# Loading a quarter of the keys onto both partition halves with one transfer, and both parts of the queries with one transfer, in a stick-breaking attention layer

## The chip, the cores and the metric

The kernel runs on one core of a Trainium2 chip. The metric is the device time of one execution in microseconds (us). The time given is the median of a few executions, and one further execution was recorded by the hardware profiler. All views quoted below are of that profiled execution.

## What is computed

One layer of a decoder trunk over 1024 tokens of width 2048, in float32. The input is normalized, multiplied by one big input matrix, and split into two groups of heads. Sixteen stick-breaking heads (`sb`) and sixteen sliding-window heads (`sw`, with four key/value heads) each attend, their outputs are normalized, gated and multiplied by one output matrix, and a normalized result is added to the input. The part that the change touches is the scores of the attention, `z = q k`:

```
u = rmsnorm(h, norm_pre)
q_sb, k_sb, v_sb, z_sb, q_sw, k_sw, v_sw, z_sw = split(u @ w_in)
# stick-breaking head:
z = einsum('bqhd,bshd->bhqs', q_blk, kh) * scale
log_1m_beta = where(before, log_sigmoid(-z), 0)
suffix = cumsum(log_1m_beta, reverse) - log_1m_beta
w = where(before, exp(log_sigmoid(z) + suffix), 0)
out = einsum('bhqs,bshd->bqhd', w, vh)
# then: o = rmsnorm(o) * silu(z), y = concat(o_sb, o_sw) @ w_out, h + rmsnorm(y)
```

## The kernel before

**The matrix engine's work.** Every float32 product is made of products of a high and a low part of each factor: a value is split into `hi` (rounded to the matrix engine's type) and `lo` (what is left), and a projection adds `hi*hi`, `hi*lo` and `lo*hi`. A projection (`proj`, L452 on) makes one block of 128 output columns of the input matrix for 1024 tokens, in four groups of weights. Each group is 256 KB, is loaded into a tile `wraw` (three buffers, L131), and is split by ScalarE (L133) and VectorE (L135). 52 projections stand in a list `work`; the attention is done in between.

**Attention between the projections.** After each three matmuls of a projection, `step()` may place one stage of one attention unit: `s1` makes the scores `z` and the weights on ScalarE, GpSimd and VectorE, `s2` transposes them on TensorE, `s3` multiplies them with the values. The places are decided while the program is written, by a running sum of matmul times (`pe_time`), with a period of 4.7 for a stick-breaking unit. A stick-breaking head has ten units: four query quarters `a`, each with the key quarters `c` from `a` to 3. A unit's transfers (`prep`) are placed when three units or fewer stand before it (`AHEAD = 3`).

**How keys and queries get onto the chip's partitions.** A projection of queries or keys leaves its high and its low part in device memory, `qd` and `kd`, each of shape [2 parts, 128 rows, 1024 tokens]; a head has 64 of the 128 rows. For the scores, TensorE works on 128 partitions at once: a query tile `q` has the high part of the queries on partitions 0 to 63 and the low part on 64 to 127. The key tiles `kh` (high part) and `kl` (low part) have the same 64 rows twice, on 0 to 63 and again on 64 to 127. One matmul with `kh` and one with `kl` then give all four products. There is one tile `kh` and one tile `kl` in the whole program; `load_k` (L478) refills a quarter, 256 tokens, at a time. It does so with four transfers: for each of the two parts, one for each partition half (L484). The stick-breaking queries come with two transfers, one for each part (L521), twice per head. The sliding-window queries (L603) come with two transfers of [64 rows, 2 heads, 256 tokens] each and are not touched by the change, but the sliding-window heads use the same `load_k`.

**What sets the order.** All these transfers are issued by the SyncE queue (SP), in program order, with the weights' loads (L131), the spills of queries and keys (L376, L377), the attention's output (L495, L497), and the background jobs. A background job (L224 to L229) loads two pieces of the output matrix into `row_sw` or `bg`, adds them on GpSimd (L227) and stores the sum `wsum`. A tile framework places the waits and, where the code does not force an order, orders each engine's instructions by its own estimates. Matmuls and background jobs are kept in the order in which they are written. The framework gives each transfer one of eight completion semaphores in turn, and a transfer first waits until the one eight before it has landed.

After the last projections comes the output stage: seven products of half-size matrices (L907), with sums and splits on the other engines. No key or stick-breaking query is loaded there.

## Time and profile before

| what | value |
|---|---|
| median of 3 runs | 1807.02 us (1804.5 to 1808.76) |
| the profiled execution | 1807.31 us |
| its span, from the first to the last instruction | 1805.6 us |
| TensorE busy in the span | 1780.6 us (99%) |
| VectorE, ScalarE, GpSimd busy | 1245.8, 789.6, 496.0 us |
| bytes moved by the DMA engines | 312.48 MB |
| matrix engine's mean granted clock | 0.998 |

In the quoted lines PE is TensorE, DVE is VectorE, ACT is ScalarE, POOL is GpSimd, and SPq is SyncE's queue, which issues the transfers. `x64` is a count. In a group's line the first pair after the bar is the total busy time in us and the mean of one in ns; after the next bar stands the idle time of the engine just before these instructions, in us, with what ended most of it. A view of windows cuts the span into stretches and gives each engine's busy time, the granted clock, and the share of its 16 DMA engines' time in which they were moving packets. "Landing" is the time at which a transfer's completion is signalled.

The stick-breaking units run from 512 us, where the first scores of pair 0 are made, to 1424 us, where the last of pair 7 are made. There are eight pairs of heads.

### The profile page before, as it was taken

Reading aid. Unit: us, or ns where it says so; the run is one execution under the profiler, and the core shown is the slowest. Engines: PE = TensorE matmul, PEld = TensorE weight load, DVE = VectorE, ACT = ScalarE, POOL = GpSimd, SP = SyncE. Lnnn points to the kernel's source line nnn. Section 1 sums busy time; section 2 is a strip of 40 time slices with the busy share of each in tenths; the row PEclk is TensorE's granted clock in tenths of the full one; section 3 lists DMA queues with packets and bytes.
Section 4 is the critical chain, followed back from the end, with each engine's and each line's share of the span. In section 5 each row is a group of like instructions: output and inputs, shape, how many; then the busy total and the mean of one; then the engine's idle time right before and its main releaser. Section 6 shows DMA issues by size and latency. Waiting matters only on the chain. (4 is left out here: it accounts for less than half of the span.)

```text
span 1805.6 us, 27329 instructions
## 1 busy us (share of the span) xinstructions
PE 1780.6 (99%) x9046; PEld 1492.2 (83%) x9046; DVE 1245.8 (69%) x1984; ACT 789.6 (44%) x1696; POOL 496.0 (27%) x648
## 2 busy tenths in 40 slices
PE   8999999999999999999999999999999999999997
PEld 7788888888888888888888888888888887888886
DVE  7558852588567688587776787767858657746867
ACT  7335531355344444344443444434435434445433
POOL 0011121211213333133232322232313225504523
PEclk9999999999999999999999999999999999999999
DMA  7548675576747657466556564454435386634485
GB/s 230 193 138 219 199 223 148 167 210 206 224 124 199 182 164 195 142 182 184 175 163 185 153 183 129 137 169 139 151 91 140 98 258 210 198 105 129 143 250 184
DMA packets 203884, 312.48 MB, mean 173 GB/s; under 512 B 24640, under 2 KB 84192, under 8 KB 203616
## 3 DMA queue, kind: packets, MB, share of 16 engines
q1 hardware_dynamic: 201680, 307.60, 57.7%
q10 hardware_dynamic: 2064, 3.15, 0.5%
q8 instruction: 72, 1.18, 0.3%
q14 instruction: 68, 0.56, 0.1%
HBM read 219.42 MB, written 91.23 MB: 172 GB/s over the span
## 5 line engine op out<-in xcount | busy, mean ns | idle before, releaser
L543 DVE TENSOR_TENSOR_SCAN m_sb<-m_sb,m_sb,zero 128x257 f32<-128x257 f32 x192 | 157.3, 857 | 46.9 <-ACT m_sb L530 46.4
L530 ACT ACTIVATE m_sb<-z_sb 128x512 f32<-128x512 f32 x160 | 96.1, 601 | 132.1 <-PE z_sb L122 119.9
L546 DVE TENSOR_TENSOR b_sb<-b_sb,m_sb 128x512 f32<-128x512 f32 x160 | 129.0, 806 | 20.5 <-POOL b_sb L536 9.0
L540 DVE TENSOR_TENSOR_SCAN m_sb<-m_sb,mask 128x256 f32<-128x256 f32 x128 | 117.4, 953 | 35.2 <-ACT m_sb L530 34.5
L907 PE MATMUL y<-wohi,x 128*128 128x512 f32 x448 | 140.8, 390 | 0.0
L562 DVE TENSOR_TENSOR wl_sb<-wt_sb,wh_sb 128x512 fp32r<-128x512 f32 (+1 forms) x160 | 100.7, 631 | 57.7 <-ACT wh_sb L561 57.0
L561 ACT CAST wh_sb<-wt_sb 128x512 fp32r<-128x512 f32 (+1 forms) x160 | 86.9, 543 | 111.6 <-PE wt_sb L126 109.3
L907 PE MATMUL y<-wohl,x 128*128 128x512 f32 x576 | 132.8, 389 | 2.7 <-DVE wohl L773 2.7
L907 PEld LDWEIGHTS y<-wohl,x 128*128 128x128 f32 x576 | 108.0, 188 | 25.5 <-DVE wohl L773 3.1
L122 PE MATMUL p_qsb<-xh,whi_qsb 128*128 128x512 f32 x256 | 104.5, 408 | 0.0
L122 PE MATMUL p_ksb<-xh,whi_ksb 128*128 128x512 f32 x256 | 104.4, 408 | 0.0
L122 PE MATMUL p_zsw<-xh,whi_zsw 128*128 128x512 f32 x256 | 104.3, 407 | 0.0
L122 PE MATMUL p_vsb<-xh,whi_vsb 128*128 128x512 f32 x256 | 102.9, 402 | 0.0
L122 PE MATMUL p_zsb<-xh,whi_zsb 128*128 128x512 f32 x256 | 102.9, 402 | 0.0
L623 ACT ACTIVATE L_sw<-L_sw,nm_sw 128x256 f32<-128x256 f32 (+1 forms) x128 | 62.6, 490 | 91.6 <-DVE nm_sw L618 88.5
L122 PE MATMUL p_zsw<-xh,wlo_zsw 128*128 128x512 f32 x256 | 101.0, 394 | 0.0
L122 PE MATMUL p_ksb<-xh,wlo_ksb 128*128 128x512 f32 x256 | 100.9, 394 | 0.0
L122 PE MATMUL p_qsb<-xh,wlo_qsb 128*128 128x512 f32 x256 | 100.8, 394 | 0.0
L122 PE MATMUL p_ksb<-xl,whi_ksb 128*128 128x512 f32 x256 | 100.7, 394 | 0.0
L122 PE MATMUL p_zsw<-xl,whi_zsw 128*128 128x512 f32 x256 | 100.7, 393 | 0.0
L122 PE MATMUL p_vsb<-xh,wlo_vsb 128*128 128x512 f32 x256 | 100.7, 393 | 0.0
L122 PE MATMUL p_qsb<-xl,whi_qsb 128*128 128x512 f32 x256 | 100.6, 393 | 0.0
(242 smaller groups left out, 4974.3 us busy)
## 6 DMA issues: line engine op xcount, KB each, us to landing
row_sw<-in_w_out SPq DMA_DIRECT2D x80, 256.0 KB, 4.2
bg<-in_w_out SPq DMA_DIRECT2D x80, 256.0 KB, 4.5
woraw<-wsum SPq DMA_DIRECT2D x80, 256.0 KB, 3.3
kh<-kd SPq DMA_DIRECT2D x160, 64.0 KB, 3.3
kl<-kd SPq DMA_DIRECT2D x160, 64.0 KB, 3.1
wsum<-row_sw SPq DMA_DIRECT2D x40, 256.0 KB, 2.6
wsum<-bg SPq DMA_DIRECT2D x40, 256.0 KB, 3.1
q_sw<-qd SPq DMA_DIRECT2D x64, 128.0 KB, 3.6
```

The costliest lines, as they stand in the source:

```text
L122: tc.keep_in_program_order(nc.tensor.matmul(ps, a, b, start=start, stop=stop))
L530: nc.scalar.activation(m[:, :, 1:257], z, AF.Sigmoid, scale=-SCALE)
L540: nc.vector.tensor_tensor_scan(m[:, tb, 1:257], m[:, tb, 1:257], mask[:, P - P * tb:P - P * tb + 256], m[:, tb, 0:1], ALU.mult, ALU.max)
L543: nc.vector.tensor_tensor_scan(m[:, tb, :], m[:, tb, :], zero.to_broadcast([P, 257]), prev[:, tb, 256:257], ALU.mult, ALU.max)
L546: nc.vector.tensor_mul(beta, beta, m[:, :, 0:256])
L561: nc.scalar.copy(wh[:, :k], pt[:, :k])
L562: nc.vector.tensor_sub(wl[:, :k], pt[:, :k], wh[:, :k].bitcast(F32))
L623: nc.scalar.activation(L[:, hh, :n], L[:, hh, :n], AF.Exp, bias=nm[:, hh:hh + 1], accum_out=sm[:, hh:hh + 1])
L907: nc.tensor.matmul(ps, xt[:, a, tcols], w[b][:, cols], start=first and n == 0, stop=last and n == 2)
```

## The change

Each quarter of each key part is now loaded by one transfer. Its source names the 64 rows twice, by an outermost step of 0 with a count of 2, and its destination is all 128 partitions. The queries of a stick-breaking head are loaded by one transfer too. Its source is the two parts of `qd`, 64 rows each, and its destination is all 128 partitions.

```
 def load_k(src, row, c):
     ...
     cols = slice(c * 256, (c + 1) * 256)
     for r in range(2):
-        for d in range(2):
-            nc.sync.dma_start(kk[r][d * HD:(d + 1) * HD, cols].bitcast(F32), src[r, row:row + HD, cols])
+        one_k = src[r, row:row + HD, cols]
+        twice = bass.AP(one_k.tensor, one_k.offset, [[0, 2]] + list(one_k.ap))
+        nc.sync.dma_start(kk[r][:, cols].bitcast(F32), twice)
...
             if a // 2 not in head:
                 qs = head[a // 2] = at.tile([P, 512], F32R, tag="q", name=f"q_{nm}")
-                for i in range(2):
-                    nc.sync.dma_start(qs[i * HD:(i + 1) * HD, :].bitcast(F32),
-                                      qd[pair][i, row:row + HD, (a // 2) * 512:(a // 2 + 1) * 512])
+                nc.sync.dma_start(qs.bitcast(F32), qd[pair][:, row:row + HD, (a // 2) * 512:(a // 2 + 1) * 512])
```

The source of a key transfer is now the access pattern [2 with step 0][64 rows with step 1024][256], that of a query transfer [2 with step 131072][64 rows with step 1024][512]; the destination is [128 partitions] in both. Before, both sides were [64 rows] or [64 partitions]. The bytes that move are the same. The program issues 1505 transfers on SP before and 1313 after: 192 fewer, 160 of them key transfers and 32 query transfers. TensorE, VectorE and GpSimd keep their instructions in the same order; on ScalarE two neighbours change places. TensorE has 97 fewer instructions that only wait, 357 instead of 454.

SP's order moves at some places, because the framework counts fewer transfers. The first is the first load of keys, for the first sliding-window group, near 80 us. Before (`kd_81` is the first spilled key block, `x2` two transfers in a row, `wraw_qsw_1` the second group of weights of a query projection):

```order
L484 DMA kh<-kd_81 64x256 x2
L484 DMA kl<-kd_81 64x256 x2
L484 DMA kh<-kd_81 64x256 x2
L484 DMA kl<-kd_81 64x256 x2
L484 DMA kh<-kd_81 64x256 x2
L131 DMA wraw_qsw_1_1014<-in_w_blk 128x512
L484 DMA kl<-kd_81 64x256 x2
L484 DMA kh<-kd_81 64x256 x2
L484 DMA kl<-kd_81 64x256 x2
L376 DMA qd_65<-hi_qsw_0_840 128x512
```

The same place after:

```order
L485 DMA kh<-kd_81 128x1x256
L485 DMA kl<-kd_81 128x1x256
L485 DMA kh<-kd_81 128x1x256
L485 DMA kl<-kd_81 128x1x256
L485 DMA kh<-kd_81 128x1x256
L485 DMA kl<-kd_81 128x1x256
L485 DMA kh<-kd_81 128x1x256
L485 DMA kl<-kd_81 128x1x256
L131 DMA wraw_qsw_1_1014<-in_w_blk 128x512
L376 DMA qd_65<-hi_qsw_0_840 128x512
```

Sixteen transfers have become eight, and the load of the weights, which stood behind ten of sixteen, now stands behind all eight. The second place is in the stick-breaking heads, where a head's first two quarters of keys are loaded (near 865 us; `wsum`, `row_sw` and `bg` belong to background jobs). Before:

```order
L131 DMA wraw_ksb_1_9545<-in_w_blk 128x512
L484 DMA kh<-kd_76 64x256 x2
L484 DMA kl<-kd_76 64x256
L229 DMA wsum_6_162<-row_sw 128x512
L484 DMA kl<-kd_76 64x256
L224 DMA row_sw<-in_w_out 128x512
L225 DMA row_sw<-in_w_out 128x512
L131 DMA wraw_ksb_2_9619<-in_w_blk 128x512
L131 DMA wraw_ksb_3_9718<-in_w_blk 128x512
L484 DMA kh<-kd_76 64x256 x2
L484 DMA kl<-kd_76 64x256 x2
```

The same place after:

```order
L131 DMA wraw_ksb_1_9443<-in_w_blk 128x512
L485 DMA kh<-kd_76 128x1x256
L485 DMA kl<-kd_76 128x1x256
L229 DMA wsum_6_162<-row_sw 128x512
L224 DMA row_sw<-in_w_out 128x512
L225 DMA row_sw<-in_w_out 128x512
L131 DMA wraw_ksb_2_9517<-in_w_blk 128x512
L131 DMA wraw_ksb_3_9611<-in_w_blk 128x512
L485 DMA kh<-kd_76 128x1x256
L485 DMA kl<-kd_76 128x1x256
```

Nothing but the number and the shape of the key transfers changes here: the store of the background job now follows the last key transfer instead of standing ahead of it, and the loads around keep their places.

## The prediction, made before the changed kernel was run

> **What bounds the kernel now.** I read the page first. Its head, its first row and its account of the DMA engines:

> ```profile
> span 1805.6 us, 27329 instructions
> ...
> PE 1780.6 (99%) x9046; PEld 1492.2 (83%) x9046; DVE 1245.8 (69%) x1984; ACT 789.6 (44%) x1696; POOL 496.0 (27%) x648
> ...
> DMA packets 203884, 312.48 MB, mean 173 GB/s; under 512 B 24640, under 2 KB 84192, under 8 KB 203616
> ## 3 DMA queue, kind: packets, MB, share of 16 engines
> q1 hardware_dynamic: 201680, 307.60, 57.7%
> q10 hardware_dynamic: 2064, 3.15, 0.5%
> ```

> TensorE is busy for 1780.6 of 1805.6 us; only 25 us can be won at all while its matmuls stay. The view of waits, for TensorE, says whom it waits for:

> ```profile
> PE f0a L122 <- ACT whi_f L308: 5.8, 1, 5.8
> PE y L907 <- DVE wohl L773: 2.7, 1, 2.7
> PE wt_sw L126 <- DVE L_sw L629: 2.4, 4, 1.1
> PE vt_vsw L126 <- DVE v_vsw L396: 1.9, 1, 1.9
> PE o_sb L122 <- DVE wl_sb L562: 1.6, 3, 0.9
> PE o_sw L122 <- ACT ot_sw L493: 0.7, 1, 0.7
> PE y L907 <- DVE wolo L773: 0.3, 1, 0.3
> PE y L907 <- DVE wolast L773: 0.2, 1, 0.2
> ```

> No line names a transfer, of keys or of anything else. The first is the start of the program; the other seven sum to 9.8 us. The remaining 9.4 us of the 25 I take for the end of the program, where the last rows are scaled and stored. The groups of the scores' matmuls, which are the readers of the changed transfers, confirm it:

> ```profile
> L122 PE MATMUL z_sb<-kl,q_sb 128*128 128x256 f32 x320 | 83.0, 281 | 0.0
> L122 PE MATMUL z_sb<-kh,q_sb 128*128 128x256 f32 x320 | 82.9, 281 | 0.0
> ```

> Idle before them is 0.0 us, though each head's first scores now follow on instructions that only wait for a key transfer. So the 97 waits that the change takes from TensorE cost nothing now.

> **The change part by part.** First what it removes. The view of the tiles gives what SP pays for an issue (minimum, median, maximum in ns):

> ```profile
> L484 SPq DMA_DIRECT2D kh<-kd x160: 444/566/2131, 79.3 to 1373.7; - x160
> L521 SPq DMA_DIRECT2D q_sb<-qd x64: 444/587/1341, 460.7 to 1376.2; - x64
> ```

> 192 issues fewer at about 0.57 us free 109 us of SP's queue. None of it is on the path: TensorE waits for no transfer. I count 0, and if the cover were gone a head would gain at most its eight key issues, 4.5 us.

> The bytes stay, so the question is how a new transfer is spread over the 16 DMA engines. The trace of before has no transfer like it. Its packet count shows what it has: 1505 transfers on SP and one on ACT, with 16 little completion packets each, are 24096; the loads of the small tables (256 rows of 32 B, 288 of 64 B) are 544 more; the sum is the 24640 under 512 B in the page, to the packet. So every transfer of before ran on all 16 engines, and every one has an outermost count of 128, 64 or 32. The new ones have an outermost count of 2 on the source side. The two halves cannot be joined into one count of 128 there, since the step between them (0 for keys, 131072 for queries) is not the step between rows. What divides a transfer by its outermost count would give each half to one engine: two engines for the whole.

> [...]

> Price of a megabyte on one engine, from the two queue rows: 57.7% of 16 engines' 1805.6 us is 16669 us for 307.60 MB, 54.2 us per MB; 0.5% is 144 us for 3.15 MB, 45.9 us per MB. A key transfer is 128 rows of 1 KB, 0.131 MB; half of it, on one engine, takes 3.0 us (by 45.9) to 3.55 us (by 54.2). A query transfer is 128 rows of 2 KB and takes 6.0 to 7.1 us on each of its two engines. A pair of heads has 16 and 4 of these: 72 to 85 us on the two engines. Now against the room there is. The view of windows, cut at the first scores of each pair; the last two columns are the share of the DMA engines' time and GB/s:

> ```profile
> 512.40:629.00 116.60, 116.60 (x626) 98.87 (x625) 82.86 (x117) 51.93 (x99) 33.33 (x59) 1.00 0.63 169
> 629.00:747.10 118.10, 116.88 (x626) 98.83 (x625) 88.90 (x117) 51.36 (x98) 40.19 (x67) 1.00 0.64 179
> 747.10:864.10 117.00, 116.61 (x625) 98.82 (x624) 85.84 (x117) 51.43 (x98) 37.08 (x63) 1.00 0.60 174
> 864.10:980.50 116.40, 116.40 (x626) 98.87 (x625) 81.80 (x113) 50.64 (x97) 35.59 (x62) 1.00 0.58 173
> 980.50:1098.60 118.10, 118.10 (x630) 99.62 (x629) 88.30 (x121) 53.57 (x101) 35.33 (x61) 1.00 0.53 153
> 1098.60:1215.00 116.40, 116.40 (x626) 98.77 (x625) 82.25 (x113) 51.39 (x96) 33.62 (x58) 1.00 0.51 152
> 1215.00:1331.40 116.40, 116.40 (x626) 98.86 (x625) 83.05 (x113) 50.49 (x96) 34.76 (x59) 1.00 0.47 142
> 1331.40:1424.90 93.50, 93.50 (x512) 79.76 (x511) 77.21 (x108) 46.84 (x89) 24.48 (x47) 1.00 0.39 104
> ```

> Share times length is what an engine is busy: 73.5, 75.6, 70.2, 67.5, 62.6, 59.4, 54.7 and 36.5 us. From each I take the old share of keys and queries (3.15 MB over 16 engines at 54.2: 10.7 us) and add 72. The two engines then need 134.8, 136.9, 131.5, 128.8, 123.9, 120.7 and 116.0 us in the first seven windows, 18.2, 18.8, 14.5, 12.4, 5.8, 4.3 and 0 us more than the windows have; the last, with one head's keys, has room. The sum is 74 us.

> Every other load has a sixteenth of its bytes on each engine, so it lands only when these two have got to it: the weights and background jobs are late with the keys. What is late next is TensorE. That it has a lead shows in SP's timeline and in TensorE's:

> ```profile
> 905.94 1.09 SPq L484 DMA_DIRECT2D kh<-kd  x2
> 907.12 1.28 SPq L484 DMA_DIRECT2D kl<-kd  x2
> ...
> 925.99 0.28 PE L122 MATMUL z_sb<-kh,q_sb 128*128 128x256 f32 x1
> ```

> A quarter of the keys is issued 20 us before its scores. Two transfers of 3.0 us leave about 14 us, spent once and refilled only in a window with room, so I don't deduct it.

> Bounds: the low end takes the other loads at 45.9 too (the old 73.5 becomes 62.8 x 0.847 = 53.2 without keys, and so on); then 8.6, 8.9, 5.4 and 3.7 us are over in four windows, 27 us in all. The high end takes the new transfers at 54.2, 13.2 us more a window: 166 us. I take the value between, since the row of q10 stems from one large transfer with little beside it, as two engines that lag behind the other fourteen have, and the rest runs in crowds as now. Earlier, in the sliding-window heads, 32 key transfers (of 3.0 us, 96 us over some 370 us) fit: I count 0. The weights moved behind eight key transfers near 80 us wait up to 24 us there, once; a few us of it may show, inside the range.

> The profiled execution took 1807.3 us, 0.3 over the median of the runs. 1807 + 74 = 1881.

> **The rivals.** *Spread over 16 engines after all.* If the division goes by the 128 partitions of the destination, or by the rows, a key transfer lands like one of the present kind:

> ```profile
> kh<-kd SPq DMA_DIRECT2D x160, 64.0 KB, 3.3
> q_sb<-qd SPq DMA_DIRECT2D x64, 128.0 KB, 3.8
> ```

> Then the SP time saved lies beside TensorE's work and the time is 1807, not slower. For it: all transfers seen use 16 engines. Against it: none seen has an outermost count below 16. It decides at 16 completion packets per new transfer.

> *Two engines, but hidden.* At the low prices and with the lead spent, 27 us shrink to 13 or nothing: 1807 to 1820. Against it: the first two windows are over by 18 us each, more than the lead.

> *More than the queue's sum, by the engines behind the loads.* GpSimd already waits for background loads, with the attention's masks behind in the same queue:

> ```profile
> 865.01 1.28 POOL L227 TENSOR_TENSOR row_sw<-row_sw 128x512 f32<-128x512 f32 x1 [8.09 <-DMA row_sw<-in_w_out]
> 866.25 1.01 POOL L536 TENSOR_SCALAR_AFFINE_SELECT b_sb<-b_sb 128x512 f32<-128x512 f32 x1
> ```

> The view of that line in the windows says how often:

> ```profile
> L227 POOL TENSOR_TENSOR bg<-bg x24: 1285/1657/1732, 531.6 to 1064.0; 128x512 f32<-128x512 f32 x24
> L227 POOL TENSOR_TENSOR row_sw<-row_sw x23: 1282/1299/1749, 546.6 to 1050.1; 128x512 f32<-128x512 f32 x23
> ...
>   DMA row_sw<-in_w_out: 47.2, 8
>   DMA bg<-in_w_out: 27.1, 8
> ```

> 16 of 47 sums wait for their load. If each waits for two key transfers more, 6 us, and all of it reaches TensorE on top of the queue's sum, that is 96 us: 1977. Against it: TensorE waiting also gives the two engines time, so the two sums overlap.

> *A gain.* All of TensorE's inner waits are 9.8 us and none is for a transfer; a reordered neighbour could win a part: 1803 at best.

> **How the numbers follow.** Two engines and a queue that overflows: 0.66, 1834 to 1973 (27 to 166 us), 1881 the likeliest. The worse sum on top: 0.08. Two engines but hidden: 0.09, half of it visible. Sixteen engines: 0.15, nearly all within 0.2%. A gain: 0.02. About 0.2%, 3.6 us, is what a measurement of this kernel can tell from no change, since its runs lie 4.3 us apart. Slower is 0.66 + 0.08 + 0.05 = 0.79, no change 0.04 + 0.14 = 0.18, faster 0.02 + 0.01 = 0.03. The range runs from 1806, which keeps most of the unchanged cases in, to 1975, the high bound; outside are the worse sum and the lower half of the unchanged cases, under 2 in 10. The likeliest case's own range is 1834 to 1973.

> **What would show it right or wrong.** Little packets under 512 B: 24640 less 192 x 16 is 21568 if a new transfer still runs on 16 engines, and 14 x 192 fewer, 18880, if on two. The landing of a key transfer should be 3.3 us if spread, and well above 6 if two engines carry a backlog, with the weights' landings up as well. TensorE's idle time should lie between 512 and 1215 us, more in the early pairs than the late ones, at scores, at projections behind late weights, and at transposes behind GpSimd. If new transfers run on two engines and the time stays, the lead or my price is wrong; if the time rises with 21568 packets, the reason is not the spread at all.

## The result and the profile after

The changed kernel takes 1970.94 us (median, 1964.73 to 1971.91) against 1805.95 us before: 1.091 times as long, interval 1.0892 to 1.0927. It is slower, as forecast, by 165 us where 74 were forecast. The head of its page and its account of the DMA engines:

```profile
span 1970.2 us, 27036 instructions
...
PE 1824.6 (93%) x9046; PEld 1521.3 (77%) x9046; DVE 1233.4 (63%) x1984; ACT 789.4 (40%) x1696; POOL 491.9 (25%) x648
...
DMA packets 198123, 312.45 MB, mean 159 GB/s; under 512 B 18880, under 2 KB 78432, under 8 KB 197856
...
q1 hardware_dynamic: 195920, 307.58, 51.1%
```

The packets under 512 B are 18880, the number that was worked out for two engines. The bytes are the same, and the price of a megabyte (51.1% of 16 engines' 1970.2 us over 307.58 MB, 52.4 us) is about the old 54.2. TensorE now idles 145.6 us instead of 25, and it is also busy 44 us longer with the same 9046 matmuls. The second part was in no term of the prediction.

The trace's completion records give the landings. In this kernel each of the 192 merged transfers leaves three records on its semaphore and each of the 1122 others 16; counted so, none of the 18528 is left over. From issue to landing, the median is now 7.2 us for `kh` and 9.2 us for `kl` (3.3 and 3.1 before), 12.2 us for the stick-breaking queries (3.8 before), and for loads that were not changed 7.0 us for `wraw_zsw` (3.7 before) and 6.9 us for `or_zsw` (4.6 before).

The view of windows cuts both kernels where the first stick-breaking scores begin and the last ones end. Columns as before: length; busy time of PE, PEld, DVE, ACT, POOL; granted clock; share of the DMA engines' time; GB/s. Before:

```profile
0.00:512.40 512.40, 501.52 (x2521) 416.93 (x2522) 329.80 (x755) 228.47 (x623) 85.85 (x76) 1.00 0.66 195
512.40:1424.20 911.80, 910.19 (x4881) 771.83 (x4880) 669.51 (x912) 406.97 (x770) 274.13 (x476) 1.00 0.55 157
1424.20:1805.60 381.40, 368.88 (x1646) 303.47 (x1645) 246.53 (x319) 154.14 (x304) 135.99 (x97) 0.99 0.58 181
```

After:

```profile
0.00:556.00 556.00, 511.61 (x2522) 423.05 (x2523) 323.70 (x755) 229.77 (x624) 85.42 (x76) 0.97 0.59 180
556.00:1585.90 1029.90, 942.07 (x4881) 792.83 (x4880) 663.44 (x911) 405.11 (x769) 271.58 (x476) 0.95 0.46 139
1585.90:1970.20 384.30, 370.96 (x1647) 305.41 (x1645) 246.26 (x320) 154.48 (x304) 134.88 (x96) 0.98 0.57 180
```

| stretch | longer by | of it TensorE idle | of it TensorE busy longer |
|---|---|---|---|
| up to the first stick-breaking scores | 43.6 us | 33.5 | 10.1 |
| the stick-breaking heads | 118.1 us | 86.2 | 31.9 |
| the output stage | 2.9 us | 0.8 | 2.1 |

The matmuls at equal counts take longer where the clock column is under 1.00: the 4881 of the stick-breaking heads are busy for 942.07 us at 0.95, against 910.19 us at 1.00 before. The trace's clock records have 20 stretches at half clock, 148 us in all, against 2 and 10.6 us before, and 19 of the 20 begin in a wait of TensorE or at most 0.4 us behind it. The waits, by whom:

```profile
PE wt_sb L126 <- DVE b_sb L545: 39.5, 12, 7.2
PE o_sb L122 <- ACT wh_sb L560: 27.6, 4, 10.8
PE o_sw L122 <- ACT ot_sw L494: 26.5, 7, 13.6
PE o_sb L122 <- DVE wl_sb L561: 20.7, 5, 8.5
PE f0a L122 <- ACT whi_f L308: 5.7, 1, 5.7
PE p_qsw L122 <- DVE u_qsw L366: 3.8, 1, 3.8
...
PE z_sw L122 <- DMA q_sw<-qd: 3.1, 2, 1.9
```

No score that waits for its keys is among them; the two waits of `z_sw`, 3.1 us in all, are for sliding-window queries. TensorE waits for ScalarE and VectorE, which wait for other loads. One such chain, from the timelines of SP, GpSimd, ScalarE and TensorE (start, length, and in brackets the idle time before):

```profile
886.52 4.69 SPq L485 DMA_DIRECT2D kl<-kd  x1
...
896.26 1.25 SPq L409 DMA_DIRECT2D or_zsw<-od  x2
...
905.15 1.26 POOL L411 TENSOR_TENSOR or_zsw<-or_zsw 128x512 f32<-128x512 f32 x1 [14.30 <-DMA or_zsw<-od]
...
906.45 0.63 ACT L431 ACTIVATE sg_zsw<-or_zsw 128x512 f32<-128x512 f32 x1 [13.21 <-POOL or_zsw L411]
906.99 0.57 ACT L560 CAST wh_sb<-wt_sb 128x512 fp32r<-128x512 f32 x1
...
907.61 0.58 PE L122 MATMUL o_sb<-wh_sb,v_vsb 128*128 128x256 f32 x1 [8.59 <-ACT wh_sb L560]
```

SP is held for 4.69 us over a single key transfer. The load of an attention output (two transfers of 256 KB) is issued ten us later and lands near 905 us, some 9 us after its issue. GpSimd adds its halves, ScalarE squares the sum, and the cast that TensorE needs stands behind that square in ScalarE's queue. An issue took 2.1 us at most for `kh` before, 1.7 for `kl` and 1.3 for `q_sb`; the rows of the tiles have up to 3.4, 5.3 and 4.6 us now, although the median fell:

```profile
L485 SPq DMA_DIRECT2D kh<-kd x80: 492/512/3399, 79.2 to 1533.1; - x80
L485 SPq DMA_DIRECT2D kl<-kd x80: 484/520/5298, 80.0 to 1533.7; - x80
L521 SPq DMA_DIRECT2D q_sb<-qd x32: 489/516/4607, 488.3 to 1534.3; - x32
```

### The profile page after: what moved, and what is told of

Same layout as the page of the kernel before. It is cut to its first block, busy times and chain, and to the rows that moved or that the text cites. A ratio compares the mean times of both kernels' runs of the same rounds, so it can differ in the third digit from the quotient of the medians.

```text
span 1970.2 us, 27036 instructions
## 1 busy us (share of the span) xinstructions
PE 1824.6 (93%) x9046; PEld 1521.3 (77%) x9046; DVE 1233.4 (63%) x1984; ACT 789.4 (40%) x1696; POOL 491.9 (25%) x648
## 2 busy tenths in 40 slices
DMA packets 198123, 312.45 MB, mean 159 GB/s; under 512 B 18880, under 2 KB 78432, under 8 KB 197856
## 3 DMA queue, kind: packets, MB, share of 16 engines
q1 hardware_dynamic: 195920, 307.58, 51.1%
q10 hardware_dynamic: 2064, 3.15, 0.4%
## 5 line engine op out<-in xcount | busy, mean ns | idle before, releaser
L542 DVE TENSOR_TENSOR_SCAN m_sb<-m_sb,m_sb,zero 128x257 f32<-128x257 f32 x192 | 148.2, 810 | 53.2 <-ACT m_sb L529 43.2
L126 PE MATMUL wt_sb<-ident,b_sb 128*128 128x128 f32 x576 | 95.7, 287 | 39.5 <-DVE b_sb L545 39.5
L906 PEld LDWEIGHTS y<-wohl,x 128*128 128x128 f32 x576 | 109.9, 191 | 27.1 <-DVE wohl L772 4.0
L126 PEld LDWEIGHTS wt_sb<-ident,b_sb 128*128 128x128 f32 x576 | 76.1, 147 | 65.9 <-DVE b_sb L545 24.5
L122 PE MATMUL o_sb<-wh_sb,v_vsb 128*128 128x256 f32 x320 | 85.5, 288 | 27.6 <-ACT wh_sb L560 27.6
L122 PE MATMUL p_qsb<-xh,whi_qsb 128*128 128x512 f32 x256 | 108.5, 424 | 0.0
L122 PE MATMUL p_zsw<-xh,whi_zsw 128*128 128x512 f32 x256 | 106.4, 416 | 0.0
L122 PE MATMUL p_ksb<-xh,whi_ksb 128*128 128x512 f32 x256 | 106.1, 415 | 0.0
L122 PE MATMUL o_sb<-wl_sb,v_vsb 128*128 128x256 f32 x320 | 86.0, 289 | 20.7 <-DVE wl_sb L561 20.7
L122 PE MATMUL p_vsb<-xh,whi_vsb 128*128 128x512 f32 x256 | 105.2, 411 | 0.0
L122 PE MATMUL p_qsb<-xl,whi_qsb 128*128 128x512 f32 x256 | 103.8, 406 | 0.0
L122 PE MATMUL p_qsb<-xh,wlo_qsb 128*128 128x512 f32 x256 | 103.5, 404 | 0.0
L122 PE MATMUL p_zsb<-xh,whi_zsb 128*128 128x512 f32 x256 | 103.5, 404 | 0.0
L122 PE MATMUL p_zsw<-xh,wlo_zsw 128*128 128x512 f32 x256 | 102.7, 401 | 0.0
L122 PE MATMUL p_zsw<-xl,whi_zsw 128*128 128x512 f32 x256 | 102.6, 401 | 0.0
## 6 DMA issues: line engine op xcount, KB each, us to landing
kh<-kd SPq DMA_DIRECT2D x80, 128.0 KB
kl<-kd SPq DMA_DIRECT2D x80, 128.0 KB
q_sw<-qd SPq DMA_DIRECT2D x64, 128.0 KB
```

Source lines behind the costliest of these rows:

```text
L122: tc.keep_in_program_order(nc.tensor.matmul(ps, a, b, start=start, stop=stop))
L126: tc.keep_in_program_order(nc.tensor.transpose(ps, a, ident))
L542: nc.vector.tensor_tensor_scan(m[:, tb, :], m[:, tb, :], zero.to_broadcast([P, 257]), prev[:, tb, 256:257], ALU.mult, ALU.max)
L906: nc.tensor.matmul(ps, xt[:, a, tcols], w[b][:, cols], start=first and n == 0, stop=last and n == 2)
```

## The experiments

The theory: a transfer's outermost count sets how many DMA engines carry it, and two engines with a backlog make every other load late. The first rival: fewer, larger transfers or the changed order of SP's queue cost the time. Within the theory two things were open: whether the two engines' total work sets the time or the engines that wait in order behind late loads do, and what the longer busy time is. Each time stands beside runs of the kernel before on the same chip; "over before" is the difference of the two medians.

**Keys alone.** Only the edit in `load_k`.

> The keys are loaded by one transfer as after, the queries by two as before. Theory (two DMA engines carry each new transfer, everything else lands behind them): packets under 512 B 24640 - 160 x 16 - 160 x 14 = 19840. The stretch before the first stick-breaking scores is as long as after, 556 us, since only keys load there; in the stick-breaking heads the two engines have 20 us less to do per pair, so the excess there falls to a third or half of the 118 us: 1880 to 1910 us in all. Rival (it is the fewer, larger transfers and the changed order of the SyncE queue that cost, not the spread): in proportion to the transfers taken away, 160 of 192, about 1943 us. Rival (my sum of the queue alone): no window overflows without the queries, so 1806 plus the 44 us of the sliding-window stretch, 1850 us.

Measured: 1880.08 us, 1.0414 (1.038 to 1.0449).

```profile
DMA packets 199083, 312.46 MB, mean 167 GB/s; under 512 B 19840, under 2 KB 79392, under 8 KB 198816
...
547.50:1492.40 944.90, 921.61 (x4881) 779.26 (x4880) 668.73 (x912) 406.49 (x770) 271.25 (x476) 0.98 0.51 152
```

The stretch up to the first stick-breaking scores is 547.5 us, 35 longer than before, and the stick-breaking heads take 944.9 us, 33 longer. In the latter the two engines have 818 us of work: the share 0.51 of 944.9 us is 482; less 6 us a pair for the keys' old sixteenth, plus 48 a pair for the new half. There is no overflow, and still 33 us are lost. That is against the queue's sum alone (1850 us). The rival that goes by the number of transfers, 1943 us, is far off too.

**Queries alone.** Only the edit in `do_prep`.

> The queries of the stick-breaking heads are loaded by one transfer as after, the keys by four as before. Theory (two engines): packets under 512 B 24640 - 32 x 16 - 32 x 14 = 23680; 24 us per pair on the two engines where there are over 40 us of room, and queries are issued 15 us or more ahead: 1806 to 1815 us, with no long stall. Rival (number and order of transfers): 32 of 192 transfers, about 1834 us.

Measured: 1829.06 us, 1.0126 (1.0104 to 1.0147).

```profile
DMA packets 202924, 312.48 MB, mean 171 GB/s; under 512 B 23680, under 2 KB 83232, under 8 KB 202656
...
514.50:1447.40 932.90, 917.91 (x4881) 774.33 (x4880) 665.09 (x912) 404.36 (x771) 272.12 (x476) 0.99 0.53 154
```

The packets are those of two engines; the 22 us are more than I allowed, again without overflow (494 less 24 plus 192 is 662 of 932.9 us). Keys alone cost 73 us and queries alone 22, 95 together; both at once cost 165. The time by itself lies near the rival's 1834; the next run decides.

**The same merged transfers over 16 engines.** Both copies of a key row, or both parts of a query row, go to neighbouring partitions, so the outermost count is 64. The last pair of lines is that of the sliding-window queries. A product over partitions does not mind their order.

```
-            twice = bass.AP(one_k.tensor, one_k.offset, [[0, 2]] + list(one_k.ap))
+            ap = list(one_k.ap)
+            twice = bass.AP(one_k.tensor, one_k.offset, [ap[0], [0, 2]] + ap[1:])
...
-                nc.sync.dma_start(qs.bitcast(F32), qd[pair][:, row:row + HD, (a // 2) * 512:(a // 2 + 1) * 512])
+                both = qd[pair][:, row:row + HD, (a // 2) * 512:(a // 2 + 1) * 512]
+                nc.sync.dma_start(qs.bitcast(F32), both.rearrange("r e t -> e r t"))
...
-                    nc.sync.dma_start(qs[r * HD:(r + 1) * HD, :, :].bitcast(F32),
+                    nc.sync.dma_start(qs[r::2, :, :].bitcast(F32),
```

> One transfer for a key quarter and one for the queries, as after, but the partitions are interleaved: row e of both copies (or both parts) goes to partitions 2e and 2e+1, so the outermost count of the source is 64 instead of 2. The sliding-window queries go to every second partition to match. What is computed is the same. Theory (two engines): packets under 512 B are 21568, all 16 engines carry each transfer, and the time is that of before, 1806 us within 4, with 192 issues fewer on SyncE. Rival (merging itself costs, by fewer completion semaphores in flight, the order of the queue or the larger transfer): stays near 1971 us.

Measured: 1805.81 us against 1807.21, 1.0000 (0.9983 to 1.0016).

```profile
span 1804.9 us, 27036 instructions
...
PE 1778.1 (99%) x9046; PEld 1492.1 (83%) x9046; DVE 1254.5 (70%) x1984; ACT 789.6 (44%) x1696; POOL 498.9 (28%) x648
...
DMA packets 200811, 312.46 MB, mean 173 GB/s; under 512 B 21568, under 2 KB 81120, under 8 KB 200544
```

As many transfers, instructions and bytes as in the changed kernel, and the whole loss is gone. Merging neither costs nor gains; the spread is the cause. The 192 issues and 97 waits saved are worth nothing here, as the prediction had it.

**As many transfers as before, on two engines.** The source of each 64-row transfer in the stick-breaking heads takes the even rows first.

```
+    def in_blocks(rows):
+        (step, n), *rest = [list(d) for d in rows.ap]
+        return bass.AP(rows.tensor, rows.offset, [[step, BLOCKS], [BLOCKS * step, n // BLOCKS]] + rest)
```

> As many transfers as before, of 64 rows each, in the sliding-window heads exactly those of before; in the stick-breaking heads the source of each key and query transfer names the even rows first and then the odd ones, an outermost count of 2. Theory (two engines): packets under 512 B 24640 - 320 x 14 = 20160, the first stick-breaking scores at 512 us as before, and the excess in the stick-breaking heads as after, about 118 us: 1925 us, 1900 to 1950. Rival (merging costs, not the spread): 1806 us.

Measured: 1915.0 us, 1.0594 (1.0564 to 1.0625), packets under 512 B 20160. Two engines without merging cost 108 us; merging on sixteen engines costs nothing. That settles the first rival. The first stick-breaking scores come at 521 us, where 512 was expected.

```profile
0.00:521.00 521.00, 501.82 (x2521) 416.44 (x2522) 328.19 (x755) 228.43 (x623) 85.58 (x76) 1.00 0.64 192
521.00:1535.10 1014.10, 940.62 (x4881) 790.14 (x4880) 660.25 (x912) 403.79 (x770) 268.13 (x476) 0.96 0.47 141
```

**Four engines.** `BLOCKS = 4`.

> As the kernel with two blocks of rows, but with four: every fourth row first, an outermost count of 4 in each key and query transfer of the stick-breaking heads, as many transfers as before. Theory (the outermost count sets how many DMA engines carry a transfer): packets under 512 B 24640 - 320 x 12 = 20800; four engines have 36 us more per pair instead of two with 72, so no window overflows, and what is left are stalls by late landings: 1806 to 1830 us. Rival (any outermost count below 16 sends the transfer through some slow path of its own): near the 1915 us of two blocks.

**Stick-breaking heads alone.** The sliding-window heads load their keys by four transfers as before.

> The changed kernel with the keys of the sliding-window heads loaded by four transfers as before. Theory (two engines, number of transfers of no account): the same as two blocks of rows, 1915 us within 12, first stick-breaking scores near 515 us, packets under 512 B 24640 - 160 x 16 - 160 x 14 + 32 x (16 + 14) = 20800 - 0, that is 24640 - 160 x 16 - 160 x 14 for all heads less the sliding-window share, with queries counted in: 128 key and 32 query transfers, 160 x 30 = 4800 fewer, 19840. The sliding-window stretch then costs 45 to 55 us of the 165. Rival (my prediction: the sliding-window heads cost nothing): 1971 us.

Measured: 1943.59 us, 1.0766 (1.0734 to 1.0797), packets under 512 B 19840 as expected; both times missed. It is 139.5 us over before where the changed kernel is 165.0, so the sliding-window heads' keys cost 26 us, not 45 to 55. The first stick-breaking scores begin at 530 us, 18 later than before: the first pair's keys, which load ahead of them from 442 us on, are still merged. And it loses 32 us more than twice as many transfers of half the size on the same two engines (107.8 us over before).

**Half the size again.** The kernel with two blocks, its transfers cut into 32 rows.

> As the kernel with two blocks of rows in the stick-breaking heads (1915 us), but each of its key and query transfers is cut into two of 32 rows: half as large, twice as many, the same packets on the same two DMA engines. Theory (a transfer waits for the one eight before it, so with smaller transfers less of the two engines' work can stand ahead of the others' loads; this is why 64-row transfers cost 28 us less than 128-row ones): faster again, 1880 to 1905 us. Rival (the two engines' total work sets the time whatever the size): 1915 us within 6, or slower by SyncE's 320 further issues.

Measured: 1903.3 us, 1.0541 (1.0508 to 1.0574). At the same work for the two engines the loss over before goes 139.5, 107.8, 97.5 us as the transfers go from 128 to 64 to 32 rows (the intervals of the last two overlap a little). That fits a limit of eight transfers ahead (in the trace of the changed kernel each of the 1306 transfers that follow another on their semaphore, one of eight, is issued after that one has landed), which lets less work stand before the others' loads when transfers are small; the limit itself was not varied, so this stays an argument.

**A lead for the background loads.** GpSimd's sums stand later behind their loads, in the changed kernel.

```
-            yield 8.0
+            yield 14.0
             BG((nc.gpsimd.tensor_add if sign > 0 ...
...
-            defer(6.0, lambda: gate(1, o1))
+            defer(12.0, lambda: gate(1, add_o(o1)))
```

> The changed kernel with its background loads given a lead: the GpSimd sum of a background job stands 14 instead of 8 us of matmul time behind its loads (with 4 and 2 instead of 6 and 6 us behind it), and the sum of the loaded attention output stands behind the projection or 12 us behind the load instead of right behind the load. Transfers and their spread as after. Theory A (late loads hold up GpSimd and, through it, ScalarE and VectorE in their order, and TensorE waits for the attention's masks and casts behind them): the waits for b_sb and wh_sb fall by half or more, and the time falls by 70 us or more, under 1900. Theory B (the two engines overflow, whoever waits first): the time falls by 20 us at most, 1950 or more.

Measured: 1942.21 us, 1.0762 (1.0726 to 1.0798): between the theories, 138 us over before where the changed kernel is 165.

```profile
PE wt_sb L126 <- DVE b_sb L548: 32.2, 9, 8.3
PE o_sb L122 <- ACT wh_sb L563: 31.6, 4, 13.1
...
560.20:1557.60 997.40, 931.93 (x4881) 785.62 (x4881) 662.30 (x912) 403.60 (x770) 274.02 (x477) 0.97 0.47 144
```

Theory A, that the waits behind GpSimd would fall by half, fell: 39.5 and 27.6 us became 32.2 and 31.6. The two engines' work explains why there was little to win. From the share: 0.47 of 997.4 is 469 us, less 9 a pair for the keys' and queries' old sixteenth (at 45.9 us per MB), plus 72 a pair on the two engines, 973 us. They are busy for 98% of the stretch; by the same sum they were busy for 978 of 1029.9 us, 95%, in the changed kernel.

**The lead where nothing overflows, and its control.**

> Only the queries by one transfer (1829 us, no overflow: the two engines need 663 of the 933 us of the stick-breaking stretch), with the lead for the background loads as in the earlier run with a lead. Theory A (without overflow, what is left is late loads that hold up GpSimd and the engines behind it): the lead takes most of the 22 us away, 1815 us or less. Rival (the 22 us come from elsewhere, such as late weights): 1825 to 1830 us.

> The control: the kernel before with the same lead for its background loads. TensorE waits for no load there, so the time should stay, 1806 us within 4. If the lead itself makes this kernel faster or slower, that difference belongs off the two runs with a lead.

Measured: 1832.48 us with queries alone, 1.0142 (1.0117 to 1.0167), and 1812.13 us for the control, 1.0042 (1.0027 to 1.0056). Theory A, 1815 us or less, fell: with the lead the loss is 27.4 us, without it 21.9. The control was not neutral either, 7.1 us slower where 4 were allowed. Its profiled execution took 1805.41 us, no more than the kernel before, so the trace does not show what those 7 us are. With them off, 20.3 us are left: the lead took away 1.5 us, less than these runs can tell from nothing. In the profiled executions (1829.65 us without the lead, 1824.71 with it, the latter 8 under its median) VectorE's waits for GpSimd's mask fall from 22.1 to 6.0 us, ScalarE's for the attention output rise from 27.5 to 34.5. Queries alone:

```profile
DVE b_sb L544 <- POOL b_sb L534: 22.1, 7, 5.0
...
ACT sg_zsw L431 <- POOL or_zsw L411: 27.5, 7, 6.5
```

With the lead:

```profile
DVE b_sb L547 <- POOL b_sb L537: 6.0, 3, 3.5
...
ACT sg_zsw L434 <- POOL or_zsw L414: 34.5, 7, 7.9
```

One wait was cured and the next in order took its place. That is seen in the waits, not in the time. Late loads reach TensorE by several engines, and no single one was shown to carry most.

**Stalls without any change of a transfer.** The kernel before, with a mask repeated on GpSimd nine times, once per head.

```
+                for _ in range(9 if a == 1 else 0):
+                    nc.gpsimd.affine_select(out=beta, in_=beta, ...)
```

> The kernel before with one stall made on purpose in each of the 16 stick-breaking heads: behind the first mask of the second query quarter GpSimd repeats the same mask nine times (the result stays the same), 9 x 0.75 = 6.7 us. No transfer is changed. If a stall of TensorE costs no more than its length, TensorE's busy time stays at 1780 us and the time rises by what TensorE idles, 16 x (6.7 - 2 us of cover) = 75 us. Theory (a stall of some us also lowers the granted clock for a while): the low stretches multiply from 2 to about 16, TensorE's busy time rises by 25 to 45 us with the same matmuls, and the time by about 110 us, 1915.

Measured: 1929.21 us, 1.0687 (1.0658 to 1.0716).

```profile
PE 1813.0 (94%) x9046; PEld 1516.4 (79%) x9046; DVE 1251.8 (65%) x1984; ACT 790.7 (41%) x1696; POOL 602.6 (31%) x792
...
PE wt_sb L126 <- DVE b_sb L549: 90.3, 16, 9.8
```

16 stalls idle TensorE 90.3 us (75 were expected), 5.6 each, and its busy time rises by 32.4 us, 2.0 per stall, with 18 stretches at half clock instead of 2. So stalls alone, with no transfer changed, bring a longer busy time with them. The clock records know only full and half, and the shortest low stretch is 3.41 us. The kernel before has one of that length, at 90 us, right behind its wait of 1.9 us for `v_vsw`. At such lengths the wait alone does not decide. The same wait of 1.9 us stands in all 14 traces and a low stretch follows it in five of them; a wait of 2.7 us in the kernel before, at 1765 us, has none. After the start of the program, every wait of 3.1 us or more in these traces, 81 in all and 15 of them in the changed kernel's, has a low stretch that begins in it or at most 3.5 us behind it.

**Short stalls.** Three repeats.

> As the kernel with nine repeated masks in each stick-breaking head, but three: 2.2 us of GpSimd work, of which about 1.1 us was covered there, so 16 stalls of TensorE of about 1.1 us. Theory (only a stall of about 2 us or more lowers the granted clock, as the gaps in the two profiles have it): TensorE idles 18 us more, its busy time stays at 1781 us within 3, and the time rises by 15 to 20 us, 1823. Rival (each stall lowers the clock, however short): busy time rises by 20 us or more, 1845.

Measured: 1812.18 us, 1.0037 (1.0021 to 1.0052).

```profile
PE wt_sb L126 <- DVE b_sb L549: 5.7, 3, 3.2
```

Both forecasts, 1823 and 1845 us, missed. Nearly all of the 2.2 us was covered: three stalls instead of sixteen. Of these, a low stretch follows the one of 3.2 us and none follows the one of 1.8 us, at 827 us. With the 1.9 us of `v_vsw` and the 2.7 us above, this is against a threshold near 2 us that decides by itself. The profiled execution took 1821.61 us, 9 over the median; apart from the start, its longest wait, 5.8 us, is in the output stage, away from the masks.

## Why the prediction was right or wrong

**The bound, and what is saved.** Right. The merged transfers over 16 engines take 1.000 times the old time; the issues and waits saved are worth 0.

**The spread.** Right, and to the packet: 18880 in the changed kernel, 21568 when interleaved, 20800 with four blocks. When it was forecast, no run had shown two engines for an outermost count of 2, since no transfer of before had such a count; the counts of packets show it. The landings came out as expected: keys land after 7.2 and 9.2 us in the median, and loads that were not changed are late as well (7.0 us for `wraw_zsw`, 3.7 before).

**The sum of 74 us.** The price and the work were near: the two engines' 978 us are 66 more than the stretch had before, where 74 were summed window by window. The step that failed is to take this overflow, 66 of the 165 us, as the whole loss. Three terms were missing or wrong:

- *The step "I count 0" for the sliding-window heads.* Their average load does fit. But keys come in bursts of eight transfers, and the stretch up to the first stick-breaking scores grew by 43.6 us: 26 go with the sliding-window heads' own keys, and the rest with the first pair's, which load there too. I had named 24 us behind the first burst alone and then let it pass as a few.
- *Late loads without overflow.* The keys alone leave the two engines at 87% of the stick-breaking stretch and cost 33 us there; the queries alone, at 71%, cost 21. In the changed kernel, 52 us of the stretch are neither old length nor overflow (1029.9 - 978). I had this mechanism as the worst rival, at 96 us and a chance of 0.08, by one route, GpSimd. The route is there, but a lead on it moved the waits to ScalarE.
- *The clock.* No term at all. It is 44 us of TensorE's busy time, over a quarter of the 165. These 44 us lie within the lengths above and do not add to them; how much would turn into idle time behind the two engines if the clock stayed full was not tried.

That 165 us lie just under the high bound of 166 is luck: the bound came from a higher price per megabyte, not from any of these terms.

**Where the stalls lie.** Half right. I expected them at scores, at projections behind late weights and at transposes behind GpSimd, less in the later pairs. None stands at a stick-breaking score or behind late weights; they stand at transposes and at the products with the values. And 33.5 us of the added idle time lie ahead of the first stick-breaking scores, where none was forecast. By the first scores of each pair, those of pairs 4 and 6, where 5.8 and 0 us were forecast, took 23.9 and 15.2 us more (1099.6 to 1241.6 and 1359.7 to 1491.3 us), about as much as the early ones, which took 17 to 23 more. Pair 5, where 4.3 us were forecast, took only 1.7 more. Why is not shown.

**The rivals.** Sixteen engines: refuted by the packets. Two engines but hidden: refuted by the time. The lead did cover the keys themselves: no stick-breaking score waits for them, though they land 7 to 9 us after their issue in the median.

What stays open is how the loss beyond the overflow divides among the engines that wait in order, and why smaller transfers on the same two engines lose less.

## What to carry to other kernels

Before two transfers are merged, look at the outermost count of the source: here a leading 2, a repeat of step 0 included, put the whole transfer on two of sixteen engines (18880 packets under 512 B, against 21568 on 16), and loads that were not changed landed later (`wraw_zsw` after 7.0 us, 3.7 before). Where the order of the partitions is free, interleave the copies so that the long count comes first: that took 1805.81 us here, against 1970.94. And when you price a stall of a saturated TensorE, price the slow clock behind it too: here 2 us for a stall of 5 to 6.

## What the runs showed of the hardware that was not expected

- In the changed kernel the issue of a transfer holds SP for up to 5.3 us for `kl`, 3.4 for `kh` and 4.6 us for `q_sb`, where 1.7, 2.1 and 1.3 us were the longest before. With the same transfers over 16 engines it is 1.3 us at most for `kh` and 0.6 for `q_sb`.
- Counting the trace's packet records from the first scores of pair 0 to those of pair 6, exactly two packets are under way for 31% of the time in the changed kernel and 2% before; with four blocks, exactly four for 15%. In the changed kernel four are under way for only 2%, which fits transfers that all use the same two engines.
- On two engines, cutting the stick-breaking transfers from 128 to 64 and 32 rows took the loss from 139.5 to 107.8 and 97.5 us, with ever more issues on SP.
- The same wait of 1.9 us of TensorE is followed by a stretch at half clock in five of 14 traces; each of the 81 waits of 3.1 us or more has one.
